# One run of filling products across both projections, with the split output weights in the places of x and h

## The chip, the cores and the metric

The kernel runs on one core of a Trainium2 chip. Its time is the device time of one execution, in microseconds (us). An execution under the profiler has a span, from the first instruction to the last, and a time of its own, somewhat longer.

The engines are named as the profile names them: PE (TensorE) for matrix products, with a granted clock that the profile shows; DVE (VectorE), ACT (ScalarE) and POOL (GpSimd) for the elementwise work; SP (SyncE), whose queue (SPq) issues nearly all DMAs here. Each engine works through its instructions in order.

## The reference

One layer of an encoder on 2048 tokens of width 1024: windowed attention with 16 query heads in 4 groups, then a SwiGLU part with 2816 hidden columns, each between two RMS norms and modulated by a vector c.

```python
mod = (c_act @ ada_w[i] + ada_b[i])[:, None, :]
sh1, sc1, g1, sh2, sc2, g2 = jnp.split(mod, 6, axis=-1)
h = rmsnorm(x, mix_norm_pre[i]) * (1.0 + sc1) + sh1
y = windowed_gqa_sink(h, att_w_qkv[j], att_w_o[j], att_sink[j], rel_bias)
x = x + g1 * rmsnorm(y, mix_norm_post[i])
h = rmsnorm(x, ffn_norm_pre[i]) * (1.0 + sc2) + sh2
y = swiglu(h, ffn_w_in[i], ffn_w_out[i])
x = x + g2 * rmsnorm(y, ffn_norm_post[i])
```

In windowed_gqa_sink, a block of 128 queries sees its own and the two neighbouring blocks of keys within 128 tokens; a learned sink logit per head joins the softmax; its output goes through w_o. All is computed to float32 accuracy: each operand is split into a high and a low part (hi, lo), and each product of two operands is three matmuls (hi by hi, hi by lo, lo by hi).

## The kernel before

Tokens come in four chunks of 512 (c = 0 to 3), each of four blocks of 128. The work has these stages.

**Front.** `Chunk` (L159) loads x of a chunk in eight tiles of 128 x 512, `squares` and `norm` make the reciprocal norm, and `h(k)` scales tile k by it (L196, DVE) and splits the result (hi L200 on ACT, lo L201 on DVE). Chunks 0 and 1 are projected to q, k and v (products psq and psv, L144 to L146) ahead of attention. `evac` (L205) takes a finished accumulator away (eq, on ACT and DVE) and SP writes it to DRAM (q_d, k_d, v_d). Between these, the modulation vector is made: `ada_load` brings a row of ada_w (tile ada, L271), `ada_reduce` (L275, DVE) multiplies it with c and sums.

**Attention.** 64 units (chunk, group, block), in the order of chunks, then groups. `Unit.scores` makes four score tiles s (L465, PE); DVE adds the bias and takes the negative row maximum nm (L468), ACT the exponential pr (L470), DVE the reciprocal rs (L472), POOL scales pr (L474). `Unit.values`, two units later (LAG), transposes pr (t, L487), splits it (phi on ACT, plo on DVE, L149 and L150) and multiplies by v (o, L492 and L493); ACT copies half of the result (low, L496), DVE adds (of, L497), SP writes it (o_d, L500). While a unit waits, PE has *filling*: products from a generator, of which `Budget.pull` (L733) draws so many per unit, FILL = 18 in units 0 to 31 and 17 in 32 to 63. `issue_after` lets them follow an instruction, here the first score of the unit before. In the first half `fill_qkv` (L503) projects chunks 2 and 3 (576 products; its weights wsr, L508, are split on ACT and POOL), and makes chunk 3's x, squares, norm and h on the way. In the second half `fillers_o` (L657) multiplies the finished attention outputs of chunks 0 to 2 by w_o: `TokenBlock` (L552) loads a block of o_d (tile ol, L558) and of x (xr, L563), splits ol, makes products py (L570 to L572), and then norms, residual and second norm (ysq, z, L576 to L584).

At unit 32 (L701 to L718) the first half's filling is drained, its pools are closed, pools for the second half are opened, and w_o is loaded in eight rows (wor, L714) and split (wo: hi on ACT, lo on DVE or POOL).

In units 8 to 31, two units of three load a row of ada_w (16 loads in all, L727), and the next unit reduces it.

**The last chunk.** `last_blocks` (L758) makes the four blocks of chunk 3's output projection, two at a time, in accumulators of the pool psC, which takes the place of attention's accumulators.

**Feed-forward.** 22 hidden tiles of 128 columns for two halves of the tokens, in seven products in place of eight for each 2 x 2 block (operands hb, ht, weights wa, ws, products pc_i, copies p_i L872), then the output products po (L1118 to L1120). It takes the rest of the time from about 790 us on.

A scheduler places the instructions: each engine's order follows a simulated timeline, in which an instruction may move ahead of where the code puts it, unless `issue_after` holds it. SP's queue keeps its order too.

Of the kernel before, what the change touches and what calls it, by code (L numbers as in the profile page):

```python
# [10 lines left out]
F32 = mybir.dt.float32  # L11
# [38 lines left out]
FILL = (18, 17)  # L50
LAG = 2

HOLD = 2
# [14 lines left out]
def encoder_layer(ctx, tc, a):  # L68
# [44 lines left out]
    def rstd_of(alloc, psp, ptag, acc, tag, r=None, direct=False):  # L113
# [8 lines left out]
        else:  # L122
            hi, lo = alloc(f"nhi{tag}")[:, :n].bitcast(F32R), alloc(f"nlo{tag}")[:, :n].bitcast(F32R)
# [28 lines left out]

    com = ExitStack()
    hs = open_pool(com, "hs", 12)
    ev = open_pool(com, "ev", 2)
    nrm = open_pool(com, "nrm")
    xs = open_pool(com, "xs", 8)

    class Chunk:  # L159


        def __init__(self, c):
            self.c, self.hh = c, [None] * KT
# [26 lines left out]
        def norm(self, psp, ptag):  # L190
            r = nrm.tile([P, CH], F32, tag="nr", name=f"nr{self.c}")
            self.r = rstd_of(rot(nrm, "nsq", 4), psp, ptag, self.acc, f"a{self.c}", r)

        def h(self, k):
            xt, c = self.xt[k], self.c
            scaled = dve.scalar_tensor_tensor(xt, xt, coef[:, 0, k:k + 1], self.r, ALU.mult, ALU.mult).ins  # L196
            hi = hs.tile([P, CH], F32R, tag="hi", name=f"hi{c}_{k}")
            lo = hs.tile([P, CH], F32R, tag="lo", name=f"lo{c}_{k}")
# [6 lines left out]
    def evac(c, n, ps, psp, ptag):  # L205

        if n < KT:
# [8 lines left out]
            dve.scalar_tensor_tensor(lo, src, DH ** -0.5, f(hi), ALU.mult, ALU.subtract)  # L216
# [27 lines left out]
    with ExitStack() as pa:  # L244
# [13 lines left out]
        cs = nrm.tile([KT, P], F32, name="cs")  # L258
# [5 lines left out]
        cb = nrm.tile([P, D], F32, name="cb")  # L264
# [91 lines left out]
        for i, n in enumerate(NORD):  # L356
# [13 lines left out]
            if i == 0:  # L370
# [7 lines left out]
                tb = nrm.tile([HEADS, CH], F32, tag="nacc", name="tb")[:, :RLEN]  # L378
# [124 lines left out]
    def fill_qkv(ch, nxt):  # L503

        for i, n in enumerate([8, 9, 10, 11] + list(range(8))):
# [12 lines left out]
            if nxt is not None:  # L518
# [33 lines left out]
    class TokenBlock:  # L552


        def __init__(self, c, b, pl=None, lo=pool):
            self.c, self.b, self.u = c, b, f"{c}_{b}"
            t = (pl or op).tile([P, 2, KT, P], F32R, tag="o", name=f"ol{self.u}", bufs=2)
            sp.dma_start(f(t[:, 1]), o_d[c][b])  # L558
            flat = t.rearrange("p s k t -> p s (k t)")
            split(flat[:, 0], flat[:, 1], f(flat[:, 1]), lo)  # L560
            self.o = t
            self.x = yq.tile([P, D], F32, tag="x", name=f"xr{self.u}", bufs=2)
            sp.dma_start(self.x, a["x"][c, b])  # L563
# [3 lines left out]
        def product(self, ps, i, k):  # L567
            w = wo_s[k][:, :, i * CH:(i + 1) * CH]
            o = self.o[:, :, k]
            pe.matmul(ps, o[:, 0], w[:, 0], start=k == 0, stop=False)  # L570
            pe.matmul(ps, o[:, 0], w[:, 1], start=False, stop=False)  # L571
            pe.matmul(ps, o[:, 1], w[:, 0], start=False, stop=k == KT - 1)  # L572
# [84 lines left out]
    def fillers_o():  # L657
        before = None
        for c in range(NCH - 1):
# [6 lines left out]
            before = turns(c, blocks) if c < CPH else None  # L666

# [26 lines left out]
    fill = Budget(fillers_qkv())  # L694
    load_qkv(0, 0)
    load_bias(0)
    oend = ExitStack()
    attn = ExitStack()
    wo_s = []
    for i, un in enumerate(units):  # L700
        if i == half:  # L701
            fill.drain()
            dve.tensor_tensor(coef[:, 1, :], mod[:, 16:24], gains[:, 1, :], ALU.mult)
            dve.scalar_tensor_tensor(coef[:, 2, :], mod[:, 32:40], 1.0, gains[:, 2, :], ALU.add, ALU.mult)
            com.close()
            wop = open_pool(oend, "wop")
            op = open_pool(oend, "op")
            yq = open_pool(oend, "yq")
            nq = open_pool(attn, "nq")
# [556 lines left out]
```

## Time and profile before

| | |
|---|---|
| times of three runs | 2108.52, 2105.21, 2102.14 us |
| median | 2105.21 us |
| the profiled execution: its time, its span | 2105.69, 2103.9 us |
| its granted PE clock, mean | 0.982 |
| stages of the span: front, attention, last chunk, feed-forward | to 173, to about 744, to 790, to 2104 us |

In the rows of a timeline stand the start, the duration, the engine, the line, the operation, the tiles (out<-in), the count, and in brackets how long the engine stood idle before and what it then waited for. A matmul's duration is longer than the distance of two matmuls, since they overlap. Rows of equal kind that follow each other are put together (x8).

### The profile page before, as it was taken

To read this page: it belongs to the slowest core of one execution; us is meant where nothing else is said; L and a number is where in the kernel's file an instruction comes from. 1 tells how busy PE (TensorE), PEld (TensorE's weight loads), DVE (VectorE), ACT (ScalarE), POOL (GpSimd) and SP (SyncE) were. 2 spreads that over 40 slices of the span, in tenths; PEclk is the share of its full clock that TensorE was granted. 3 is DMA by queue.
4 is the path that set the end of the run, shared out by engine and by line. 5 is a ranking of instruction groups with operands and counts; after the bars stand their busy time and mean duration, and the time that the engine had idled before them with its cause. 6 is when DMAs were issued, how large, how long until landed. Compare 5 with 4: busy or idle time off the path is not lost.

```text
span 2103.9 us, 28722 instructions
## 1 busy us (share of the span) xinstructions
PE 2025.3 (96%) x9400; PEld 1668.0 (79%) x9400; DVE 1504.8 (72%) x2616; ACT 1012.0 (48%) x2121; POOL 967.2 (46%) x930
## 2 busy tenths in 40 slices
PE   8999989989999999999999999999999999999998
PEld 5787777878878777888788887888888778877886
DVE  7755686677677668555575698777875689987677
ACT  4425666676777656333333344434333654435222
POOL 0305544555446543555555456555453242395340
PEclk9999999999999999999999999999999999999999
DMA  8788767764546575444642454544434454469763
GB/s 304 218 255 254 219 190 235 225 196 155 191 150 220 184 250 201 141 136 145 221 140 97 158 179 149 194 145 181 159 146 160 166 183 139 129 249 364 265 247 123
DMA packets 256405, 403.21 MB, mean 192 GB/s; under 512 B 84677, under 2 KB 135413, under 8 KB 254208
## 3 DMA queue, kind: packets, MB, share of 16 engines
q1 hardware_dynamic: 248992, 380.33, 54.2%
q10 hardware_dynamic: 5792, 16.79, 2.0%
q0 software_dynamic: 1472, 4.27, 0.5%
q8 instruction: 74, 1.21, 0.2%
q14 instruction: 75, 0.61, 0.1%
HBM read 268.36 MB, written 132.95 MB: 191 GB/s over the span
## 4 chain that ended last, share of the span: by engine, by line
PE 74%; DVE 9%; DMA 6%; POOL 4%; issue 3%; ACT 3%; SPq 1%; ACTq 0%; DVEq 0%; POOLq 0%
PE pc_i L145 12%; PE pc_i L146 12%; PE pc_i L144 12%; PE po L1119 5%; PE po L1120 5%; PE po L1118 5%; PE psq L144 3%; PE psq L146 3%; PE psq L145 3%; PE py L570 2%; PE py L571 2%; PE py L572 2%; PE t L487 2%; PE s L465 2%; DMA ada<-ada_w 1%
## 5 line engine op out<-in xcount | busy, mean ns | idle before, releaser
L146 PE MATMUL pc_i<-ht,ws_i 128*128 128x512 f32 x528 | 206.5, 391 | 0.0
L145 PE MATMUL pc_i<-ht,ws_i 128*128 128x512 f32 x528 | 206.4, 391 | 0.0
L144 PE MATMUL pc_i<-ht,ws_i 128*128 128x512 f32 x528 | 205.6, 390 | 0.0
L474 POOL TENSOR_SCALAR pr<-pr,rs 128x288 f32<-128x288 f32 (+3 forms) x256 | 131.8, 534 | 138.8 <-DVE rs L472 134.7
L470 ACT ACTIVATE pr<-pr,nm 128x289 f32<-128x289 f32 (+3 forms) x256 | 135.0, 529 | 76.7 <-DVE nm L468 66.2
L149 ACT CAST wa_i<-wiri 128x512 fp32r<-128x512 f32 x132 | 81.8, 621 | 182.0 <-PE pc_i L146 150.4
L468 DVE CUSTOM_DVE_ANT_0 pr<-s,bias,nsink 128x288 f32<-128x288 f32 (+3 forms) x256 | 124.4, 499 | 60.5 <-PE s L465 47.8
L808 POOL TENSOR_TENSOR s_i<-wiri 128x512 f32<-128x512 f32 x44 | 61.3, 1392 | 202.4 <-DMA wiri<-w_in 183.7
L150 DVE TENSOR_TENSOR ws_i<-s_i,ws_i 128x512 fp32r<-128x512 f32 x132 | 114.1, 864 | 40.9 <-ACT ws_i L149 40.6
L145 PE MATMUL pc_i<-hb,wa_i 128*128 128x512 f32 x352 | 138.5, 394 | 0.0
L150 DVE TENSOR_TENSOR plo<-t,phi 128x512 fp32r<-128x512 f32 x184 | 121.5, 681 | 23.3 <-ACT phi L149 23.0
L146 PE MATMUL pc_i<-hb,wa_i 128*128 128x512 f32 x352 | 138.1, 392 | 0.0
L144 PE MATMUL pc_i<-hb,wa_i 128*128 128x512 f32 x352 | 137.3, 390 | 0.0
L465 PE MATMUL s<-k,q 128*128 128x288 f32 (+4 forms) x512 | 112.1, 318 | 19.2 <-DVE nm L468 18.0
L150 DVE TENSOR_TENSOR wa_i<-wiri,wa_i 128x512 fp32r<-128x512 f32 x132 | 118.7, 900 | 15.3 <-ACT wa_i L149 14.8
L1118 PE MATMUL po<-wo_s,g 128*128 128x512 f32 x320 | 124.8, 394 | 4.8 <-ACT wo_s L149 4.0
L1119 PE MATMUL po<-wo_s,g 128*128 128x512 f32 x320 | 126.3, 395 | 3.1 <-DVE wo_s L150 3.1
L149 ACT CAST ws_i<-s_i 128x512 fp32r<-128x512 f32 x132 | 81.8, 620 | 98.3 <-PE pc_i L146 91.7
L1120 PE MATMUL po<-wo_s,g 128*128 128x512 f32 x320 | 125.9, 394 | 0.0
L487 PE MATMUL t<-ident,pr 128*128 128x128 f32 x736 | 112.6, 277 | 9.9 <-POOL pr L474 4.1
L1126 DVE TENSOR_TENSOR z<-po,z 128x512 f32<-128x512 f32 x140 | 94.4, 684 | 30.5 <-PE po L1120 29.0
L145 PEld LDWEIGHTS pc_i<-ht,ws_i 128*128 128x128 f32 x528 | 99.1, 188 | 21.6
(249 smaller groups left out, 6026.5 us busy)
## 6 DMA issues: line engine op xcount, KB each, us to landing
wiri<-w_in SPq DMA_DIRECT2D x88, 512.0 KB, 4.6
ada<-ada_w SPq DMA_DIRECT2D x40, 512.0 KB, 6.8
wr<-w_out SPq DMA_DIRECT2D x20, 1024.0 KB, 7.2
g<-g_d_t SPq DMA_DIRECT2D x36, 512.0 KB, 5.7
g<-g_d_b SPq DMA_DIRECT2D x35, 512.0 KB, 5.5
q_d<-eq SPq DMA_DIRECT2D x64, 256.0 KB, 4.8
q<-q_d SPq DMA_DIRECT2D x16, 1024.0 KB, 5.7
wsr<-w_qkv SPq DMA_DIRECT2D x24, 512.0 KB, 5.4
```

The costliest lines, as they stand in the source:

```text
L144: pe.matmul(ps, w[0], h[0], start=first, stop=False)
L145: pe.matmul(ps, w[0], h[1], start=False, stop=False)
L146: pe.matmul(ps, w[1], h[0], start=False, stop=last)
L149: act.copy(hi, src)
L150: return eng.tensor_tensor(lo, src, f(hi), ALU.subtract).ins
L465: m = pe.matmul(ps[:, :n], qs, kk[:, e, jb * P + lo:jb * P + hi], start=e == 0, stop=e == 1)
L470: act.activation(pr[:, i, lo:hi + 1], pr[:, i, lo:hi + 1], AF.Exp, bias=nm[:, i:i + 1], scale=-1.0, accum_out=rs[:, i:i + 1])
L474: pool.tensor_scalar(pr[:, i, lo:hi], pr[:, i, lo:hi], rs[:, i:i + 1], 1.0, ALU.mult, ALU.mult)
L487: pe.transpose(pt[:, i * P:(i + 1) * P], pr[:, i, jj * P:(jj + 1) * P], ident)
L1118: pe.matmul(ps, g[:, 0], w[:, 0], start=k == 0, stop=False)
L1119: pe.matmul(ps, g[:, 0], w[:, 1], start=False, stop=False)
L1120: pe.matmul(ps, g[:, 1], w[:, 0], start=False, stop=k == m - 1)
```

## The change

- **Places.** The pools xs (x) and hs (h) stay open after the first half. x of a chunk lies in two tiles of four, h in pairs (12 of them). The split output weights take these places: of w_o's columns 0 to 511 (half 0) four rows of tiles go where x was and four into h's pairs; of columns 512 to 1023 (half 1) all go into h's pairs. The pool op, opened at the start, first holds the squares, the norm and c's row.
- **When.** `output_weights` loads and splits half 0, a step per unit from unit 24 on. `filling` is one generator for both halves: the projection of chunks 2 and 3, then half 1's weights, then `fillers_o`. So there is no drain at unit 32. FILL is 17.9 everywhere; products follow the first score of two units before (SLACK = 2).
- **ada.** The 16 loads go out in units 8 to 23, one each; a row is reduced when two are outstanding, the older first.
- **Scalings.** Those of chunk 3 are held behind the evacuation just made (newest["evac"]).
- **Last chunk.** Its blocks 0 and 1 are loaded into tiles of their own (apart) behind units 62 and 63, and become filling; `last_blocks` makes blocks 2 and 3 only. `TokenBlock` loads x when the block's first product is evacuated (`begin`).

The core of the diff:

```diff
-FILL = (18, 17)
+FILL = 17.9
 LAG = 2
-
-HOLD = 2
+SLACK = 2
+HOLD = 1
...
-            self.xt = [xs.tile([P, CH], F32, tag="x", name=f"x{c}_{k}") for k in range(KT)]
+            groups = [xs.tile([P, 4, CH], F32, tag="x", name=f"x{c}_{i}") for i in range(2)]
+            self.xt = [groups[k // 4][:, k % 4] for k in range(KT)]
...
-                    nxt.h(2 * i - 16)
-                    nxt.h(2 * i - 15)
+                    with tc.issue_after(newest["evac"]):
+                        nxt.h(2 * i - 16)
+                        nxt.h(2 * i - 15)
...
+            if apart:
+                t = [nq.tile([P, D], F32, tag="n", name=f"ol{self.u}_{i}", bufs=5).bitcast(F32R) for i in range(2)]
+            else:
+                t = op.tile([P, 2, D], F32R, tag="o", name=f"ol{self.u}")
+                t = [t[:, 0], t[:, 1]]
+            sp.dma_start(f(t[1]), o_d[c][b].rearrange("p k t -> p (k t)"))
+            split(t[0], t[1], f(t[1]), lo)
+            self.o = [i.rearrange("p (k t) -> p k t", k=KT) for i in t]
...
+        for x in final:
+            yield from x.fill()
+
+    def proj_raw(i, m):
+        raw = ada_late.tile([P, D], F32, tag="raw", name=f"wor{i}_{m}").rearrange("p (e c) -> p e c", e=2)
+        sp.dma_start(raw, a["w_o"][2 * m:2 * m + 2, :, i * CH:(i + 1) * CH].rearrange("e p c -> p e c"))
+        return i, m, raw
+
+    def proj_split(i, m, raw):
+        if i == 0 and m < 2:
+            w = xs.tile([P, 4, CH], F32, tag="x", name=f"wo{i}_{m}").bitcast(F32R)
+            split(w[:, :2].rearrange("p e c -> p (e c)"), w[:, 2:].rearrange("p e c -> p (e c)"),
+                  raw.rearrange("p e c -> p (e c)"), dve)
+            for e in range(2):
+                wo_s[i, 2 * m + e] = (w[:, e], w[:, 2 + e])
+            return
+        for e in range(2):
+            w = hs.tile([P, 2, CH], F32R, tag="h", name=f"wo{i}_{m}_{e}")
+            split(w[:, 0], w[:, 1], raw[:, e], (dve, pool)[e])
+            wo_s[i, 2 * m + e] = (w[:, 0], w[:, 1])
+
+    def output_weights():
+        raws_ = [proj_raw(0, 0), proj_raw(0, 1)]
+        yield
+        for i in range(4):
+            proj_split(*raws_.pop(0))
+            if i < 2:
+                raws_.append(proj_raw(0, 2 + i))
+            yield
 
...
+    def filling():
+        nonlocal yq, nq, g1row
+        yield from fillers_qkv()
+        dve.tensor_tensor(coef[:, 1, :], mod[:, 16:24], gains[:, 1, :], ALU.mult)
+        dve.scalar_tensor_tensor(coef[:, 2, :], mod[:, 32:40], 1.0, gains[:, 2, :], ALU.add, ALU.mult)
+        raws_ = [proj_raw(1, m) for m in range(2)]
+        for m in range(2, 4):
+            proj_split(*raws_.pop(0))
+            raws_.append(proj_raw(1, m))
+        for x in raws_:
+            proj_split(*x)
+        com.close()
+        yq = open_pool(oend, "yq")
+        nq = open_pool(attn, "nq")
+        g1row = yq.tile([P, D], F32, name="g1row")
+        make_row(coef[:, 1, :], g1row, yq.tile([P, CH], F32, tag="sq", name="growt0", bufs=1), 0)
+        yield from fillers_o()
...
-        if waiting:
-            ada_reduce(*waiting.pop())
-        if KT <= i < half and i % 3 != 1:
+        if len(waiting) > 1:
+            ada_reduce(*waiting.pop(0))
+        if KT <= i < 3 * KT:
             with tc.issue_after(newest["wsr"]):
                 waiting.append(ada_load(next(late_ada), ada_late))
+        elif waiting:
+            ada_reduce(*waiting.pop(0))
+        elif 3 * KT <= i < half:
+            next(weights, None)
...
-        fill.pull(FILL[i >= half], units[max(i - 1, 0)].first)
+        if i >= len(units) - LAG:
+            final.append(TokenBlock(NCH - 1, len(final), True))
+        fill.pull(FILL, units[max(i - SLACK, 0)].first)
...
-    last_blocks(range(2), op)
...
-    last_blocks(range(2, JB), op2)
+    last_blocks(range(LAG, JB))
```

What this does to the engines' orders at three places. The first is DVE where chunk 3's norm ends (nr before, normed after), in the middle of attention; x_0 to x_7 are that chunk's x, nm and pr belong to scores, plo and of to values. Before:

```order
L136 TENSOR_TENSOR nr_2819<-nr_2819,nta_2827 128x512
L150 TENSOR_TENSOR plo_2_2_2791<-t_2_2_2785,phi_2_2_2790 128x512
L196 SCALAR_TENSOR_TENSOR x_0_2310<-x_0_2310,coef,nr_2819 128x512
L196 SCALAR_TENSOR_TENSOR x_1_2311<-x_1_2311,coef,nr_2819 128x512
L196 SCALAR_TENSOR_TENSOR x_2_2312<-x_2_2312,coef,nr_2819 128x512
L196 SCALAR_TENSOR_TENSOR x_3_2313<-x_3_2313,coef,nr_2819 128x512
L196 SCALAR_TENSOR_TENSOR x_4_2314<-x_4_2314,coef,nr_2819 128x512
L196 SCALAR_TENSOR_TENSOR x_5_2315<-x_5_2315,coef,nr_2819 128x512
L196 SCALAR_TENSOR_TENSOR x_6_2316<-x_6_2316,coef,nr_2819 128x512
L196 SCALAR_TENSOR_TENSOR x_7_2317<-x_7_2317,coef,nr_2819 128x512
L468 ISA pr_1780,nm_2_2743<-s_2_1_2751,bias_1893,nsink 128x288
L468 ISA nm_2_2743 128x1
```

After, where x_0 and x_1 are tiles of four:

```order
L283 ISA ada_3109,mod<-ada_3109,normed,adab 128x1024
L283 ISA mod 128x1
L135 SCALAR_TENSOR_TENSOR squared<-nsta_2741,squared 128x512
L136 TENSOR_SCALAR squared<-squared 128x512
L225 SCALAR_TENSOR_TENSOR eq_2_2935<-psq_4_2758,eq_2_2935 128x16x32
L137 TENSOR_TENSOR normed<-normed,squared 128x512
L476 ISA pr_1714,nm_2_2566<-s_2_1_2574,bias_1828,nsink 128x288
L476 ISA nm_2_2566 128x1
L476 ISA pr_1714,nm_2_2566<-s_2_2_2579,bias_1828,nsink 128x288
L476 ISA nm_2_2566 128x1
L205 SCALAR_TENSOR_TENSOR x_0_2245<-x_0_2245,coef,normed 128x512 x2
L505 TENSOR_TENSOR of_1_2532<-o_1_2497,low_1_2531 64x4x128
```

Eight scalings in one run have become pairs, with scores' and values' rows between them; a reduction of ada (L283) stands among them.

The second is PE at units 31 to 33, where the filling passes from one projection to the other (t, s and o are attention's, py_0_0 is the first block of the output projection). Before, in units 32 and 33:

```order
L487 MATMUL t_3_2_5089<-ident,pr_1779 128x128 x4
L465 MATMUL s_0_2_5040<-k_0_4593,q_0_4591 128x288 x2
L465 MATMUL s_0_3_5045<-k_0_4593,q_0_4591 128x288 x2
L465 MATMUL s_0_0_5135<-k_0_4593,q_0_4591 128x288 x2
L465 MATMUL s_0_1_5140<-k_0_4593,q_0_4591 128x288 x2
L465 MATMUL s_0_2_5145<-k_0_4593,q_0_4591 128x288 x2
L487 MATMUL t_3_0_5162<-ident,pr_1780 128x128 x4
L465 MATMUL s_0_3_5150<-k_0_4593,q_0_4591 128x288 x2
L487 MATMUL t_3_1_5173<-ident,pr_1780 128x128 x4
L465 MATMUL s_0_0_5225<-k_0_4593,q_0_4591 128x288 x2
L492 MATMUL o_3_5066<-phi_3_0_5072,v_3_4198 128x512
```

After, in unit 31:

```order
L584 MATMUL py_0_0_5028<-wo_2_1_4535,ol_0_5024 128x512
L495 MATMUL t_3_0_4830<-ident,pr_1716 128x128
L585 MATMUL py_0_0_5028<-wo_2_1_4535,ol_0_5024 128x512
L586 MATMUL py_0_0_5028<-wo_2_1_4535,ol_0_5024 128x512
L584 MATMUL py_0_0_5028<-wo_3_0_4633,ol_0_5024 128x512
L473 MATMUL s_3_2_4813<-k_3_4121,q_3_4119 128x288 x2
L585 MATMUL py_0_0_5028<-wo_3_0_4633,ol_0_5024 128x512
L586 MATMUL py_0_0_5028<-wo_3_0_4633,ol_0_5024 128x512
L584 MATMUL py_0_0_5028<-wo_3_1_4636,ol_0_5024 128x512
L473 MATMUL s_3_3_4818<-k_3_4121,q_3_4119 128x288 x2
L585 MATMUL py_0_0_5028<-wo_3_1_4636,ol_0_5024 128x512
L495 MATMUL t_3_1_4841<-ident,pr_1716 128x128
```

Before, attention's own rows follow each other without a product; after, products stand between them.

The third is PE at the end of attention: the last values (o_3), and the last chunk's blocks (py_0_0 and py_0_1 of block 0, py_1_0 of block 1). Before:

```order
L570 MATMUL py_3_1_8464<-wo_5024,ol_3_8428 128x512
L571 MATMUL py_3_1_8464<-wo_5024,ol_3_8428 128x512
L493 MATMUL o_3_8340<-plo_3_0_8347,v_3_7510 128x512
L572 MATMUL py_3_1_8464<-wo_5024,ol_3_8428 128x512
L492 MATMUL o_3_8340<-phi_3_1_8357,v_3_7510 128x512
L493 MATMUL o_3_8340<-plo_3_1_8358,v_3_7510 128x512
L570 MATMUL py_0_0_8559<-wo_4989,ol_0_8543 128x512
L571 MATMUL py_0_0_8559<-wo_4989,ol_0_8543 128x512
L572 MATMUL py_0_0_8559<-wo_4989,ol_0_8543 128x512
L570 MATMUL py_0_1_8560<-wo_4989,ol_0_8543 128x512
```

After:

```order
L584 MATMUL py_0_1_8476<-wo_3_0_5001,ol_0_0_8155 128x512
L500 MATMUL o_3_8346<-phi_3_0_8352,v_3_7475 128x512
L501 MATMUL o_3_8346<-plo_3_0_8353,v_3_7475 128x512
L500 MATMUL o_3_8346<-phi_3_1_8363,v_3_7475 128x512
L501 MATMUL o_3_8346<-plo_3_1_8364,v_3_7475 128x512
L585 MATMUL py_0_1_8476<-wo_3_0_5001,ol_0_0_8155 128x512
L586 MATMUL py_0_1_8476<-wo_3_0_5001,ol_0_1_8156 128x512
L584 MATMUL py_0_1_8476<-wo_3_1_5004,ol_0_0_8155 128x512
L585 MATMUL py_0_1_8476<-wo_3_1_5004,ol_0_0_8155 128x512
L586 MATMUL py_0_1_8476<-wo_3_1_5004,ol_0_1_8156 128x512
L584 MATMUL py_1_0_8527<-wo_0_4328,ol_1_0_8253 128x512
L585 MATMUL py_1_0_8527<-wo_0_4328,ol_1_0_8253 128x512
```

Block 0 stood behind the last values before; now it stands ahead of them, and 29 products, the rest of block 0 and all of block 1's first accumulator, stand between them and block 2.

More of the change, by code (lines that the diff above doesn't have):

```diff
@@ L150, in split, with square_at @@
         return eng.tensor_tensor(lo, src, f(hi), ALU.subtract).ins
+    oend = ExitStack()
     com = ExitStack()
-    hs = open_pool(com, "hs", 12)
+    xs = open_pool(oend, "xs", 2)
+    hs = open_pool(oend, "hs", 12)
+    op = open_pool(oend, "op", 2)
     ev = open_pool(com, "ev", 2)
-    nrm = open_pool(com, "nrm")
-    xs = open_pool(com, "xs", 8)
+    squared = op.tile([P, 4, CH], F32, tag="o", name="squared")
+    normed = op.tile([P, 4, CH], F32, tag="o", name="normed")
+    cb = normed.rearrange("p a b -> p (a b)")[:, :D]
+    turn_of_square = iter(range(10 ** 6))
+    def square_at():
+        return squared[:, next(turn_of_square) % 4]
     class Chunk:
@@ L567, in product @@
         def product(self, ps, i, k):
[L568 to L572, printed above, removed]
+            w = wo_s[i, k]
+            hi, lo = (t[:, k] for t in self.o)
+            pe.matmul(ps, hi, w[0], start=k == 0, stop=False)
+            pe.matmul(ps, hi, w[1], start=False, stop=False)
+            pe.matmul(ps, lo, w[0], start=False, stop=k == KT - 1)
         def evac(self, ps, i):
+            if i == 0:
+                self.begin()
             sq = yq.tile([P, CH], F32, tag="sq", name=f"ysq{self.u}_{i}", bufs=1)
@@ L693, in encoder_layer @@
     half, done = len(units) // 2, 0
-    fill = Budget(fillers_qkv())
     load_qkv(0, 0)
     load_bias(0)
-    oend = ExitStack()
     attn = ExitStack()
-    wo_s = []
-    for i, un in enumerate(units):
[L701 to L709, printed above, removed]
-            g1row = yq.tile([P, D], F32, name="g1row")
-            make_row(coef[:, 1, :], g1row, yq.tile([P, CH], F32, tag="sq", name="growt0", bufs=1), 0)
-            for k in range(KT):
-                raw = yq.tile([P, D], F32, tag="z", name=f"wor{k}", bufs=3)
-                sp.dma_start(raw, a["w_o"][k])
-                w = wop.tile([P, 2, D], F32R, name=f"wo{k}")
-                split(w[:, 0], w[:, 1], raw, (dve, pool)[k % 2])
-                wo_s.append(w)
-            fill = Budget(fillers_o())
+    wo_s, final = {}, []
+    def filling():
[15 more added lines that the diff above has]
+        yield from fillers_o()
+    yq = nq = g1row = None
+    fill = Budget(filling())
+    weights = output_weights()
+    for i, un in enumerate(units):
         un.scores()
@@ L756, in temp, with last_blocks @@
         return tmp.tile([P, CH], F32, tag=tag, name=name, bufs=bufs)
-    def last_blocks(bs, pl):
-        blocks = [TokenBlock(NCH - 1, b, pl) for b in bs]
+    def last_blocks(bs):
+        blocks = [TokenBlock(NCH - 1, b) for b in bs]
         ps = {(x, i): psC.tile([P, CH], F32, tag="p", name=f"py{x.u}_{i}") for x in blocks for i in range(2)}
```

32 lines of the change are left out of this document (13 added, 19 removed).

## The prediction, made before the changed kernel had run

> **What bounds the kernel now.** I read the page's first part, then the list of waits of TensorE (PE), then PE's timeline at each of its longer pauses up to 820 us, and beside it the engine that ended the pause.
>
> ```profile
> span 2103.9 us, 28722 instructions
> ...
> PE 2025.3 (96%) x9400; PEld 1668.0 (79%) x9400; DVE 1504.8 (72%) x2616; ACT 1012.0 (48%) x2121; POOL 967.2 (46%) x930
> ```
>
> PE is the bound: the next engine, VectorE (DVE), is busy for 72%. The change leaves the number of products as it is, so it can only win or lose what PE spends beside them: 78.6 us of pauses (2103.9 less 2025.3), and what its clock loses. The first row of PE's waits (columns: us in total, times, longest) says that scores waiting for DVE's row maxima are the largest of these:
>
> ```profile
> PE s L465 <- DVE nm L468: 18.0, 13, 5.3
> ```
>
> A pause costs more than itself when the clock falls behind it. PE's timeline behind two pauses:
>
> ```profile
> 468.10 0.41 PE L487 MATMUL t<-ident,pr 128*128 128x128 f32 x2 [1.08 <-DVE rs L472]
> ...
> 469.28 0.40 PE L570 MATMUL py<-wo,ol 128*128 128x512 f32 x1
> 469.51 0.39 PE L571 MATMUL py<-wo,ol 128*128 128x512 f32 x1
> ...
> 744.07 0.80 PE L570 MATMUL py<-wo,ol 128*128 128x512 f32 x1 [4.62 <-DVE of L497]
> ...
> 745.09 0.63 PE L572 MATMUL py<-wo,ol 128*128 128x512 f32 x1
> 745.52 0.63 PE L570 MATMUL py<-wo,ol 128*128 128x512 f32 x1
> ...
> 749.79 0.56 PE L571 MATMUL py<-wo,ol 128*128 128x512 f32 x1
> ```
>
> At full clock products start 0.23 us apart (469.28, 469.51). Behind 744.07 they start 0.43 apart (745.09, 745.52) until 749.79: 5.7 us for work of 5.7 × 0.23 / 0.43 = 3.1. So this pause cost 4.6 + 2.6 = 7.2 us. Where slow products follow for a shorter stretch I charge half of that surcharge, 1.3, as an estimate.
>
> **The change part by part.** Chunk 3's scaling by its norm comes first. What DVE did, and PE's pause:
>
> ```profile
> 265.09 7.48 DVE L196 SCALAR_TENSOR_TENSOR x<-x,coef,nr 128x512 f32<-128x512 f32 x8
> ...
> 273.06 0.85 PE L465 MATMUL s<-k,q 128*128 128x288 f32 x2 [5.26 <-DVE nm L468]
> ...
> 276.44 0.63 PE L145 MATMUL psq<-lo,ws 128*128 128x512 f32 x1
> ```
>
> Eight scalings (7.48 us) stand ahead of one row maximum, PE waits 5.26 and is still slow (0.63 for a product) at 276.44: 5.3 + 2.6 = 7.9 us. The change holds each pair of scalings behind an evacuation, and DVE now has them two at a time, 2 × 0.94 = 1.9 us. Of the run of eight PE covered 7.48 − 5.26 = 2.2, more than a pair's 1.9. So I take all 7.9 as gain; if two of the four pairs still meet a maximum without that cover, for 1.9 each at most, it is 4.1.
>
> The late loads of modulation weights (tile ada) stop PE twice:
>
> ```profile
> 341.78 1.28 DVE L275 CUSTOM_DVE_ANT_0 ada<-ada,cb,adab 128x1024 f32<-128x1024 f32 x1 [2.87 <-DMA ada<-ada_w]
> ...
> 343.57 0.56 PE L465 MATMUL s<-k,q 128*128 128x288 f32 x2 [3.48 <-DVE nm L468]
> ...
> 401.43 2.44 DVE L275 CUSTOM_DVE_ANT_0 ada<-ada,cb,adab 128x1024 f32<-128x1024 f32 x1 [1.30 <-DMA ada<-ada_w]
> ...
> 404.37 0.53 PE L465 MATMUL s<-k,q 128*128 128x288 f32 x2 [2.36 <-DVE nm L468]
> ```
>
> DVE, which works in order, sits at a reduction whose load has not landed; behind it stand row maxima, and PE waits for these. Price: 3.5 + 1.3 = 4.8, and 2.4 + 1.3 = 3.6, together 8.4 us. Now the same 16 loads go out in 16 consecutive units, and two are outstanding before one is reduced, which helps. But in the new order the reductions still float ahead on DVE, and SyncE's queue gets more waits: ada loads that need a buffer which DVE must free stand ahead of chunk 3's key writes, of attention's outputs and of four output-weight loads in units 17 to 20. All that SyncE sends is behind such a load, the next group's q, k and v too, and DVE and PE wait for that. Bounds: no stop (a gain of 8.4), or five at 4.8 (a loss of 15.6). I take one stop, 4.8, the nearest row: gain 3.6.
>
> The hand-over between the projections: before, no product is drawn in units 31 to 33, while the output weights are split and PE has only attention's work. PE there, beside the 1.08 at 468.10 above:
>
> ```profile
> 460.49 1.09 PE L487 MATMUL t<-ident,pr 128*128 128x128 f32 x4 [2.60 <-DVE plo L150]
> ```
>
> With one slow stretch that is 2.6 + 1.1 + 1.3 = 5.0 us. In the new order 23 products stand in each of units 31 to 33, and three in unit 30. The splits, on ACT, DVE and POOL, go from the hole to units 18 to 31, under full filling. I leave 1.5 for the short unit 30: gain 3.5 (bounds 5.0, and 0 if the splits there delay a maximum as much as here).
>
> The end of attention stays thin: before, units 61 and 62 draw no product; after, 61 draws six and 62 none.
>
> ```profile
> 698.55 0.44 PE L487 MATMUL t<-ident,pr 128*128 128x128 f32 x2 [2.03 <-POOL pr L474]
> ...
> 705.38 0.45 PE L465 MATMUL s<-k,q 128*128 128x160 f32 x2 [1.68 <-DVE nm L468]
> 705.67 0.62 PE L570 MATMUL py<-wo,ol 128*128 128x512 f32 x1
> ```
>
> 2.0 + 1.7, with a surcharge at each, are 6.3 us. As 48 products more are drawn ahead of this stretch and the hole itself is only a little shorter, I take 2.0 as gain (0 to 6.3). The product at 705.67 is slow (0.62) behind a pause of 1.68. [...]
>
> The last chunk: before, its block 0 waits at 744.07 for an accumulator that DVE's last attention output frees; DVE waits for ACT, and ACT, in order, for a block's load.
>
> ```profile
> 717.06 0.58 SPq L500 DMA_DIRECT2D o_d<-of  x1
> ...
> 725.75 1.07 ACT L149 CAST ol<-ol 128x1024 fp32r<-128x1024 f32 x1
> ...
> 739.95 1.04 ACT L149 CAST ol<-ol 128x1024 fp32r<-128x1024 f32 x1 [4.14 <-DMA ol<-o_d]
> ```
>
> As filling, blocks 0 and 1 use the filling's accumulators, and 29 products (29 × 0.235 = 6.8 us) lie between the last values and block 2's first product, more than the 4.62 it waited. Late next is block 0's own load: from the write at 717.06 to the end of the cast at 726.82 are 9.8 us, and the new order has some 45 products (10.5 us) between its unit's last values and its own first product, with the evacuation ahead of the write still to come off. I leave 1.5 (0 to 4.6): gain 7.2 − 1.5 = 5.7.
>
> The start of the feed-forward part, and chunk 1's norm at the front of the kernel:
>
> ```profile
> 77.42 0.59 PE L127 MATMUL nsta<-nloa,ones 128*128 128x512 f32 x1 [1.45 <-DVE nloa L125]
> ...
> 812.16 0.79 PE L144 MATMUL pc_i<-hb,ws_i 128*128 128x512 f32 x1 [4.99 <-ACT p_i L872]
> ```
>
> At 812.16 the order on PE is the old one, blocks 2 and 3 still end just before, and ACT's copy p_i stands behind the same work and six weight casts: I give 1.0 (bounds −2 and 5). At 77.42 the norm's product moves behind more products of the first wave, but x, now grouped in larger tiles, is loaded later: 2.0 of 1.45 + 1.3 (bounds −2 and 2.8).
>
> What no row shows: waits of ACT for output-weight loads in units 18 to 31, of PE for half 1's weights, of loads for buffers that hold x or h. They can't be below zero, since each is new; above, by the stop at 343.57, 4.8 in each of three places, 14.4. I take one, 4.8, since each has two units or more of work as cover.
>
> Sum: 7.9 + 3.6 + 3.5 + 2.0 + 5.7 + 1.0 + 2.0 − 4.8 = 20.9. The profiled execution took 2105.7 us, 1.8 around its span, and 0.5 above the median of the runs shown: 2105.7 − 20.9 = 2085.
>
> **The rivals.** A is the forecast, 2085.
>
> B: the hand-over and the end give nothing. For it: the pauses at 460.49, 468.10, 698.55 and 705.38 end with DVE and POOL, whose work per unit stays, and block 0's own load may be as late as the accumulator was. Against it: elsewhere, with 18 products in a unit, such pauses are short; of the 18.0 us in 13 waits for maxima the four quoted make 12.8, and the other nine 0.6 each. Then 3.5, 2.0 and 5.7 go: 2096.
>
> C, slower: SyncE's queue is held in units 8 to 31 by loads whose buffer is freed by a reduction or a split that is itself behind attention's work on DVE. The forecast counts two stops of 4.8. It is even at 20.9 / 4.8 = 4.4 stops more, slower by over 0.3% from six more; with ten in these 24 units it is 2085 + 8 × 4.8 = 2123. For it: one load in every unit where before two in three had one, and wo's loads behind them in the same queue. Against it: of 16 such loads two stopped PE before, and a second outstanding load gives each one unit more.
>
> D: the new waits don't come, and ada never stops PE: 20.9 + 4.8 + 4.8, and 3.0 of what is left in unit 30 and for block 0, is 33.5: 2072.
>
> That the change doesn't do what it says is excluded for filling and scalings by the order of instructions.
>
> **How the numbers follow.** A 0.64, B 0.17, C 0.07, D 0.12. The likeliest gives 2085. About 0.3%, 6.3 us, is what a measurement of this kernel can tell from no change; so 2099 is the line. A and D lie below it but for a little of A (its unknown costs at their upper end), and of B some two thirds: faster 0.84. Same is the rest of B, and some of A: 0.09. Slower is C: 0.07. The range reaches from D, with 2 more of the end's bound, to a little beyond B: 2070 to 2101.
>
> **What would show it.** Right: no run of eight scalings on DVE and no pause over 2 us near 273; no pause of PE over 1.5 us in units 31 to 33; block 2's first product without a wait for attention's accumulator; at most one stop over 3 us behind a reduction of ada. Wrong: scores waiting for row maxima still at 15 us or more in sum, with reductions or splits waiting for loads just ahead; a wait of over 4 us for block 0's load; a pause at the first products of half 1's weights; or a first wave that waits for x.

## The result, and the profile after the change

The change made the kernel slower, where the prediction had it faster. The changed kernel takes 2121.43 us, median of 5 runs (2114.2 to 2123.55); the kernel before takes 2105.21 (2102.14 to 2108.52). The ratio is 1.0067, 95% interval 1.0043 to 1.0091. The profiled execution took 2115.18 us, 1.9 of it around its span. Of all executions here, one of e3's twelve below stands apart at 6184.57 us, and its ratio is made without it. The page's first part:

```profile
span 2113.3 us, 28683 instructions
...
PE 2016.2 (95%) x9400; PEld 1661.8 (79%) x9400; DVE 1506.2 (71%) x2620; ACT 1009.4 (48%) x2127; POOL 969.9 (46%) x932
```

PE has the same 9400 products and is still the bound. What it spends beside them grew from 78.6 us to 97.1 (2113.3 − 2016.2).

Five of PE's waits in the changed kernel (us in total, times, longest):

```profile
PE nsta L127 <- DVE nhla L125: 15.0, 1, 15.0
PE pc_i L145 <- ACT p_i L925: 13.0, 2, 10.6
PE s L473 <- DVE nm L476: 9.5, 10, 2.9
PE t L495 <- DVE plo L151: 6.6, 2, 3.4
PE py L584 <- ACT ol L150: 3.1, 1, 3.1
```

Scores waiting for row maxima, the largest wait before, fell from 18.0 to 9.5. Two waits took their place that are not in attention at all: one of 15.0 at chunk 1's norm (1.45 before) and one of 10.6 at the start of the feed-forward part (4.99 before).

Where that leaves the time can be read from PE's first product of each stage, in us from the span's start:

| | before | after | stage longer or shorter |
|---|---|---|---|
| first score (front ends) | 171.9 | 190.7 | +18.8 |
| first feed-forward product (attention and last chunk end) | 790.4 | 795.7 | −13.5 |
| its 97th product | 820.6 | 830.9 | +5.0 |
| end of the span | 2103.9 | 2113.3 | −0.9 |

These rows add up to 9.4 us between the two profiled executions; the medians are 16.2 apart, since the changed kernel's profiled execution was the second fastest of five. Attention and the last chunk gave 13.5 of the 17.9 us that the prediction's terms for them make (7.9 + 3.6 + 3.5 + 2.0 + 5.7 − 4.8). The front took 18.8, and the start of the feed-forward part 5.0.

**The front.** PE and DVE in the changed kernel, where chunk 1's norm is made:

```profile
100.06 1.28 DVE L283 CUSTOM_DVE_ANT_0 ada<-ada,normed,adab 128x1024 f32<-128x1024 f32 x1 [5.97 <-DMA ada<-ada_w]
...
101.40 0.43 DVE L125 CAST nhla<-normed 128x512 fp32r<-128x512 f32 x1
...
101.88 0.79 PE L127 MATMUL nsta<-nhla,ones 128*128 128x512 f32 x1 [15.00 <-DVE nhla L125]
...
106.74 0.63 PE L146 MATMUL psq<-h,w 128*128 128x512 f32 x1
107.71 0.39 PE L146 MATMUL psq<-h,w 128*128 128x512 f32 x1
```

The sum of squares is cast into the tile nhla at 101.40; PE waits 15.0 us for that, and its products are slow (0.63 each, starting 0.43 us apart, at a granted clock of 0.50) until 107.4, 5.5 us; at the distance of 0.23 that they have from 107.48 on (clock 1.00), that is an estimated surcharge of 2.6. Together that is 17.6, where the kernel before waited 1.45: some 16 of the front's 18.8. SyncE's queue ahead of it:

```profile
74.71 7.46 SPq L238 DMA_DIRECT2D k_d<-e  x8
82.27 11.18 SPq L230 DMA_DIRECT2D q_d<-eq  x8
93.54 0.91 SPq L279 DMA_DIRECT2D ada<-ada_w  x1
94.55 3.22 SPq L346 DMA_DIRECT2D v_d<-e_v  x4
```

In the diff, `rstd_of` takes nhla (its two halves) as a tile of the tag "e" from the pool of evacuations. That tag has two buffers, which the keys and values of the first wave use in turn. The buffer that nhla gets is the one of the first values (e_v), and it is free when the first two of the writes v_d have read it; these are issued from 94.55 on, since eight key writes and eight query writes stand ahead of them, 18.6 us of issuing, and land 5.6 us after their issue (median of the four). A reduction of ada, whose load stands in the same place of the queue, ends on DVE just ahead of the cast, at 101.34; so in this run two late transfers end almost together.

**The start of the feed-forward part.** PE and ACT in the changed kernel, and then its SyncE queue:

```profile
815.74 0.62 ACT L150 CAST wa_i<-wiri 128x512 fp32r<-128x512 f32 x1 [2.20 <-DMA wiri<-w_in]
...
820.19 0.62 ACT L150 CAST ws_i<-s_i 128x512 fp32r<-128x512 f32 x1 [1.67 <-POOL s_i L862]
...
822.80 0.57 ACT L925 COPY p_i<-pc_i 128x512 f32<-128x512 f32 x1
823.42 0.80 PE L145 MATMUL pc_i<-hb,ws_i 128*128 128x512 f32 x1 [10.65 <-ACT p_i L925]
```

```profile
789.31 6.63 SPq L577 DMA_DIRECT2D xr<-x  x2
796.04 7.35 SPq L845 DMA_DIRECT2D ht<-hd_d_t  x12
803.90 5.02 SPq L845 DMA_DIRECT2D hb<-h_d  x4
809.02 0.38 SPq L856 DMA_DIRECT2D wiri<-w_in  x1
```

The same place in the queue of the kernel before:

```profile
766.93 0.33 SPq L803 DMA_DIRECT2D wiri<-w_in  x1
...
782.29 5.27 SPq L563 DMA_DIRECT2D xr<-x  x2
787.65 8.43 SPq L792 DMA_DIRECT2D ht<-hd_d_t  x12
```

Hidden tile 1's weights (wiri) were sent for at 766.93, 15 us ahead of x and the operands of the first level. In the changed kernel they stand behind all of these, at 809.02 (why was read from the code alone: the operands' loads have a raised priority, and the weights' memory seems to come free later). On ACT their casts are ahead of the copy p_i, and PE waits 10.65 for that copy.

**Attention.** The pairs of scalings, POOL and PE at two places of the changed kernel (of the other two pairs, the one at 299.61 reads the same, with 3.53; the one at 281.46 takes 2.68):

```profile
309.40 3.81 DVE L205 SCALAR_TENSOR_TENSOR x<-x,coef,normed 128x512 f32<-128x512 f32 x2
309.86 2.80 POOL L151 TENSOR_TENSOR ws<-wsr,ws 128x1024 fp32r<-128x1024 f32 x1
...
315.17 0.76 PE L495 MATMUL t<-ident,pr 128*128 128x128 f32 x4 [3.20 <-DVE plo L151]
...
323.62 3.51 DVE L205 SCALAR_TENSOR_TENSOR x<-x,coef,normed 128x512 f32<-128x512 f32 x2
324.00 2.58 POOL L151 TENSOR_TENSOR ws<-wsr,ws 128x1024 fp32r<-128x1024 f32 x1 [0.61 <-ACT ws L150]
```

Three of the four pairs take 3.5 to 3.8 us and not 1.9: POOL's split of a weight tile starts inside it. PE has no wait at 273 any more, but 3.20 and 3.40 us soon behind two of the pairs.

**The last chunk.** ACT and PE at its third block:

```profile
769.90 1.06 ACT L600 ACTIVATE xr<-z 128x1024 f32<-128x1024 f32 x1 [6.53 <-DVE z L599]
...
775.86 1.04 ACT L150 CAST ol<-ol 128x1024 fp32r<-128x1024 f32 x1
...
776.96 0.80 PE L584 MATMUL py<-wo,ol 128*128 128x512 f32 x1 [3.13 <-ACT ol L150]
```

The wait of 4.62 for an accumulator is gone. A wait of 3.13 for block 3's own operand has come: its cast stands on ACT behind an activation that waited 6.53 for DVE.

### The profile page after: what moved, and what is told of

It is laid out like the page before. It is cut to its first block, busy times and chain, and to the rows that moved or that the text cites. A ratio compares the mean times of both kernels' runs of the same rounds, so it can differ in the third digit from the quotient of the medians.

```text
span 2113.3 us, 28683 instructions
## 1 busy us (share of the span) xinstructions
PE 2016.2 (95%) x9400; PEld 1661.8 (79%) x9400; DVE 1506.2 (71%) x2620; ACT 1009.4 (48%) x2127; POOL 969.9 (46%) x932
## 4 chain that ended last, share of the span: by engine, by line
PE 66%; DMA 6%; DVE 5%; POOL 3%; issue 2%; ACT 2%; SPq 0%; DVEq 0%; POOLq 0%; ACTq 0%
PE pc_i L147 12%; PE pc_i L146 12%; PE pc_i L145 12%; PE po L1170 4%; PE po L1171 4%; PE po L1169 4%; PE t L495 3%; PE s L473 2%; PE py L584 2%; PE py L586 2%; PE py L585 2%; PE o L500 1%; PE o L501 1%; DMA wr<-w_out 1%; PE psq L145 1%
## 5 line engine op out<-in xcount | busy, mean ns | idle before, releaser
L146 PEld LDWEIGHTS pc_i<-ht,ws_i 128*128 128x128 f32 x528 | 99.4, 188 | 21.6
L145 PEld LDWEIGHTS pc_i<-ht,ws_i 128*128 128x128 f32 x528 | 99.4, 188 | 21.5
```

Of the source, the lines that this page charges most:

```text
L145: pe.matmul(ps, w[0], h[0], start=first, stop=False)
L146: pe.matmul(ps, w[0], h[1], start=False, stop=False)
```

## Experiments

The letters stand for theories. H: the halves' place in the evacuations' buffers costs the front its 15 us and what follows. W: the weights of hidden tile 1, behind other loads, cost the feed-forward part's start. S: the scalings' pairs collide with POOL's splits, so that spreading them gains nothing. A: reductions of ada that wait on DVE for their loads cost more than the few long stops show. X: x loads of the last chunk, ahead in SyncE's queue, make block 3's operand late. The expectations set rivals against them. Each ratio is to runs of the kernel before on the same chip; e1 to e4, e5 to e8 and e9 to e12 ran on three chips, so runs of different groups are compared by their ratios.

**e1, the halves in buffers of their own** (the changed kernel, otherwise as it is):

```diff
-            halves = ev.tile([P, 2, CH], F32R, tag="e", name=f"nhl{tag}")
-            hi, lo = halves[:, 0], halves[:, 1]
+            hi = ev.tile([P, CH], F32R, tag="nhi", name=f"nhi{tag}", bufs=1)
+            lo = ev.tile([P, CH], F32R, tag="vt", name=f"nlo{tag}", bufs=1)
```

> The changed kernel, with the two halves of the chunk norm's sum of squares in tiles of their own in place of a pair that rotates with the key and value evacuations (tag e). Theory H (the halves wait for a place that the value writes of chunk 0 free, and these stand in SP's queue behind eight query writes): PE's pause of 15.0 us at chunk 1's norm falls under 2 us, the slow clock behind it goes, and the time falls by 14 to 18 us, to about 2105. Rival R (the pause comes from the grouped x tiles, or from the reduction of ada that DVE does just ahead): the pause stays above 8 us, and the time within 6 us of the changed kernel's 2121.

2103.39 us (2096.37 to 2107.3), ratio to the kernel before 0.9989 (0.9976 to 1.0001). PE has no wait for the norm's halves left; the first score comes at 174.4 instead of 190.7. One tile's place was worth 16 us at the first score, and without it the loss of time is gone. The front stays 2.5 us later than before the change.

**e4, the reverse: the kernel before, with only the halves' tile moved to "e"**:

```diff
-            hi, lo = alloc(f"nhi{tag}")[:, :n].bitcast(F32R), alloc(f"nlo{tag}")[:, :n].bitcast(F32R)
+            halves = ev.tile([P, 2, CH], F32R, tag="e", name=f"nhl{tag}")
+            hi, lo = halves[:, 0], halves[:, 1]
```

> The kernel before with one part of the change alone: the halves of the norm's sum rotate with the key and value evacuations. Theory H: chunk 1's norm stops PE for 10 us or more (1.45 in the kernel before), and the time rises by 10 to 18 us, to about 2119. Rival R (grouped x tiles or the reductions): no pause over 4 us there, and the time stays within 5 us of 2105.

2123.19 us (2118.63 to 2125.05), ratio 1.0075 (1.0046 to 1.0104). The first score comes at 189.9 (171.9 before), and PE's row:

```profile
101.58 0.80 PE L127 MATMUL nsta<-nhla,ones 128*128 128x512 f32 x1 [17.43 <-DVE nhla L125]
```

This edit alone, without the new ada loads or the tiles of four, makes 16 to 18 us (by the ratio and by the medians). That the tile's place costs this is shown from both sides. What holds the cast, once the place is taken, is two things at once: three reductions of ada, which stood behind the cast in the kernel before (it at 73.83, they from 96.25), stand ahead of it in e4 and end at 101.01, and the second write that frees the buffer lands at 101.0. In the changed kernel too both end together. The place brings both, and no run parts them.

**e2, hidden tile 1's weights sent for ahead of the operands** (the changed kernel):

```diff
+    with tc.high_priority(offset=100):
+        ahead["i0_1"] = raw_load(wi[1], K2, "i0_1", a["w_in"][1], a["w_in"][HT + 1])
     with tc.high_priority(offset=100):
         half.load("t3", "t1", "t4", "b22")
```

> The changed kernel, with the weight load of the second hidden tile issued ahead of the twelve ht and four hb loads at the start of the feed-forward part. Theory W (ACT's copy p_i stands behind casts of weights whose load SP issues only after these): PE's pause before the first product that waits for p_i falls from 10.65 to 5 us or less, as in the kernel before, and the time by 4 to 6 us, to about 2116. Rival: the weights' sums on POOL, or the copy's place on ACT, keep the pause above 8 us, and the time stays at 2121.

2112.42 us (2110.14 to 2118.52), ratio 1.0041 (1.0025 to 1.0057). PE at the feed-forward part's start:

```profile
805.43 0.49 PE L145 MATMUL pc_i<-ht,ws_i 128*128 128x512 f32 x1 [2.12 <-ACT ht L150]
...
807.70 0.73 PE L146 MATMUL pc_i<-ht,ws_i 128*128 128x512 f32 x1 [1.77 <-DVE ht L151]
...
822.54 0.80 PE L145 MATMUL pc_i<-hb,ws_i 128*128 128x512 f32 x1 [3.02 <-ACT p_i L933]
```

The wait for p_i fell from 10.65 to 3.02, as W says, but the operands (ht), now behind the weights, are waited for instead: the first 96 products take 36.6 us, 35.2 in the changed kernel and 30.2 before. So the place of the weights made that one wait, but the stage is no shorter without it (35.2 to 37.6 us in the changed kernel, e1 and e12, which lack this edit): what lengthens it by 5.0 stays open. The interval overlaps the changed kernel's (1.0043 to 1.0091); that e2 is faster is likely, not shown.

**e3, e1's and e2's edits together** (the repaired kernel from here on):

> Both edits in the changed kernel: halves of their own, and the second hidden tile's weights ahead. If both theories hold, the two costs add: 2121 less 16 less 5 is 2100, some 5 us below the kernel before. By the rival of the first the time stays above 2112.

2100.53 us median (eleven of its twelve executions from 2096.38 to 2110.36), ratio 0.9978 (0.9963 to 0.9993): faster than the kernel before by 0.2%. By its stages attention and the last chunk take 602.1 us (780.4 − 178.3), 16.4 less than before: nearly the 17.9 forecast. The front is 6.4 later, the first 96 feed-forward products 5.5 longer. Two stops behind reductions of ada that the changed kernel didn't have are here (in e1 too, 4.51 and 3.93). DVE's and PE's rows:

```profile
293.99 2.38 DVE L283 CUSTOM_DVE_ANT_0 ada<-ada,normed,adab 128x1024 f32<-128x1024 f32 x1 [4.06 <-DMA ada<-ada_w]
...
298.72 0.72 PE L473 MATMUL s<-k,q 128*128 128x160 f32 x2 [4.51 <-DVE nm L476]
...
345.87 3.37 DVE L283 CUSTOM_DVE_ANT_0 ada<-ada,normed,adab 128x1024 f32<-128x1024 f32 x1 [4.99 <-DMA ada<-ada_w]
...
349.73 1.09 PE L473 MATMUL s<-k,q 128*128 128x288 f32 x3 [4.04 <-DVE nm L476]
```

**e5, the kernel before, with only the scalings in pairs behind an evacuation**:

```diff
+                    with tc.issue_after(newest["evac"]):
+                        nxt.h(2 * i - 16)
+                        nxt.h(2 * i - 15)
```

> The kernel before with one part of the change alone: chunk 3's scalings held behind the evacuations, two at a time. The prediction's term: the pause of 5.26 us at 273 and its slow stretch go, the time falls by 7.9 us, to about 2097. Theory S (a scaling reads two tiles from memory and stands still while POOL splits a weight tile, which comes beside each evacuation: pairs took 3.8 and 3.5 us in the changed kernel, where two free ones take 1.4 to 1.5): two or more pairs take over 2.6 us, PE pauses of 2 to 3.5 us stand there in place of the one, and the time falls by no more than 4 us.

2105.45 us (2096.25 to 2113.51), ratio 1.0008 (0.9994 to 1.0022). The largest term of the sum, 7.9 us, is nothing when made alone. Three of its pairs take 3.5 us or more, the last 1.39. DVE and POOL at the first:

```profile
271.74 3.56 DVE L196 SCALAR_TENSOR_TENSOR x<-x,coef,nr 128x512 f32<-128x512 f32 x2
272.12 2.62 POOL L150 TENSOR_TENSOR ws<-wsr,ws 128x1024 fp32r<-128x1024 f32 x1 [0.33 <-ACT ws L149]
```

The pair is slow beside POOL here too. The wait of 5.26 at 273 goes; waits of 1.92 (280.48) and 1.89 (292.02) stand between the pairs, one of 3.20 (260.25) 11 us ahead of the first, and the waits at attention's end are longer (3.10 and 2.73, where 2.03 and 1.68 were). That the slow pairs alone eat up the gain is therefore not shown.

**e6, the repaired kernel, the low parts of these weight tiles on DVE instead of POOL**:

```diff
-            split(w[:, 0], w[:, 1], raw, pool)
+            split(w[:, 0], w[:, 1], raw, dve if nxt is not None and i >= 8 else pool)
```

> The repaired kernel of the run with both edits, with the low parts of the four weight tiles beside these scalings made by DVE in place of POOL. Theory S: no scaling of chunk 3 takes over 1.0 us any more (2.83 us for a pair before), though DVE has four splits of about 1.2 us more; the time falls by 1 to 4 us from 2100. Rival (the long pairs come from something else, such as the loads): pairs of over 2.6 us remain.

2094.17 us (2091.58 to 2098.46), ratio 0.9955 (0.9942 to 0.9968). The first, second and fourth of its pairs (the third takes 1.65), and the split that POOL still makes beside the fourth:

```profile
265.87 1.41 DVE L205 SCALAR_TENSOR_TENSOR x<-x,coef,normed 128x512 f32<-128x512 f32 x2
281.17 1.41 DVE L205 SCALAR_TENSOR_TENSOR x<-x,coef,normed 128x512 f32<-128x512 f32 x2
...
305.48 3.51 DVE L205 SCALAR_TENSOR_TENSOR x<-x,coef,normed 128x512 f32<-128x512 f32 x2
305.86 2.59 POOL L151 TENSOR_TENSOR ws<-wsr,ws 128x1024 fp32r<-128x1024 f32 x1 [1.65 <-ACT ws L150]
```

1.41 to 1.65 where no split of POOL's runs beside, 3.5 where one does, in the same run: the collision is shown, though the expectation that no scaling is slow any more was missed. e3's four pairs took 2.83, 1.40, 1.40 and 3.51; at its second it was POOL's split, begun after the pair, that took longer (3.48). So the edit shortened one pair, by 1.4 us, and the gain of some 5 us has another part that wasn't found: the stops of 4.51 and 4.04 behind reductions aren't in e6's profile either. The interval touches e3's (0.9963 to 0.9993), and e10 below gains nothing from the same edit.

**e7, the repaired kernel, each reduction of ada held on DVE behind the last row maximum of its unit**:

```diff
-            ada_reduce(*waiting.pop(0))
+            with tc.issue_after(un.last):
+                ada_reduce(*waiting.pop(0))
```

> The repaired kernel with each late reduction of ada held behind the last row maximum of its unit, so that it can't move ahead to units before. Theory A of the prediction (a reduction that stands ahead of row maxima and waits for its load stops PE): the pauses of 4.5 us at 299 and 4.0 us at 350 and their slow stretches go, and the time falls by 6 to 12 us, to 2088 to 2094. Rival: a reduction waits as long behind the last maximum and stops the next unit's, so that pauses of 3 us or more remain, and the time stays within 3 us of 2100.

2082.51 us (2081.49 to 2085.95), ratio 0.9898 (0.9886 to 0.9911): by the ratios some 17 us below e3, well over the 6 to 12 expected. DVE's wait for these loads (us in total, times, longest) in e3 and then in e7:

```profile
DVE ada L283 <- DMA ada<-ada_w: 23.6, 12, 5.0
```

```profile
DVE ada L283 <- DMA ada<-ada_w: 13.4, 5, 5.2
```

The stops of 4.51 and 4.04 are gone; one of 3.02 remains, at 301.81, for plo. The work of each engine in attention's first half (stretch, its length; busy us and instructions of PE, PEld, DVE, ACT, POOL; granted clock; DMA share; GB/s), in e3 and then in e7:

```profile
175.00:465.00 290.00, 269.28 (x1402) 224.09 (x1401) 207.36 (x499) 192.89 (x465) 165.10 (x231) 0.96 0.73 218
```

```profile
175.00:465.00 290.00, 279.38 (x1473) 231.99 (x1473) 211.85 (x522) 200.98 (x488) 156.19 (x237) 0.98 0.77 229
```

In the same 290 us e7 gets 71 matmuls more done, at a granted clock of 0.98 instead of 0.96. Part of that is a front that ends 4.4 us sooner (the first score at 173.9, 178.3 in e3). The stretch from 310 to 440 us shows the rest best: 706 matmuls for 658, PE idle for 1.6 us and not 6.7, at a clock of 1.00 for 0.96.

**e9, the kernel before, with reductions held in the same way**:

> The kernel before, with each late reduction of ada held behind the last row maximum of its unit, and nothing else. Theory A: the two pauses of 3.48 and 2.36 us (8.4 us with their slow stretches) go, and the time falls by 5 to 9 us, to about 2097; as the repaired kernel fell by 18 us with the same edit, this says how much of that belongs to the change's own denser loads. Rival: the reductions wait behind the maxima instead, and the time stays within 3 us of 2104.

2090.54 us (2087.68 to 2091.38), ratio 0.9926 (0.9909 to 0.9943): 14.8 us. The prediction priced everything that ada cost this kernel at 8.4, by its two long stops. That holding the reductions back is worth more is shown, in both kernels. DVE's wait for the loads in the kernel before, and then in e9:

```profile
DVE ada L275 <- DMA ada<-ada_w: 25.3, 11, 3.6
```

```profile
DVE ada L275 <- DMA ada<-ada_w: 14.4, 6, 4.2
```

The two long stops (343.57 and 404.37) are gone. From 310 to 440 us e9 does 718 matmuls for 669, with PE idle for 1.4 us and not 5.8, at a clock of 1.00 for 0.97; at that pace 49 matmuls are some 9 us, about what the two stops were priced at. The other 6 of the 14.8 couldn't be put down to a wait: PE's waits for maxima make 19.1 us in 13 times in e9, 18.0 in 13 before, with new ones of 2.92 and 2.90 (264.64, 268.39) in the place of 5.26, and of 5.52 (452.31) at the hand-over.

**e8, the repaired kernel, the last chunk's x loads on POOL's queue**:

```diff
-            sp.dma_start(self.x, a["x"][self.c, self.b])
+            (pool if self.c == NCH - 1 else sp).dma_start(self.x, a["x"][self.c, self.b])
```

> The repaired kernel with the last chunk's x loads issued by POOL's queue in place of SP's. Theory X (the load of x for the last chunk's block 1, which moved to the first evacuation, waits for a buffer at the head of SP's queue, and the last attention output's write and block 3's load stand behind it): the pause of 3.3 us at block 3's first product goes, and the time falls by 3 to 6 us, to 2095 to 2098. Rival: the load or its cast on ACT is late on its own, and the pause stays over 2 us.

2099.14 us (2097.06 to 2103.61), ratio 0.9978 (0.9967 to 0.9989), as e3. ACT and PE at block 3:

```profile
756.65 1.06 ACT L600 ACTIVATE xr<-z 128x1024 f32<-128x1024 f32 x1 [6.54 <-DVE z L599]
...
762.00 1.04 ACT L150 CAST ol<-ol 128x1024 fp32r<-128x1024 f32 x1
...
763.09 0.50 PE L584 MATMUL py<-wo,ol 128*128 128x512 f32 x1 [3.41 <-ACT ol L150]
```

X has fallen: the wait is as long (3.41) with the x loads out of the way. The cast's place behind the activation that waits 6.54 for DVE, and behind seven other casts, is what is left; it was only read from the rows, no run moved it.

**e10, e7 with e6's edit; e11, e10 with e8's; e12, the changed kernel once more**, on one chip with e9:

> The repaired kernel with both the reductions held behind the last maximum and the low parts of the four weight tiles on DVE. If the two costs are apart, 2100 less 18 less 6 is 2076; if the shorter pairs of scalings only helped because reductions stood beside them, it stays at 2082.

> As the run before, and the last chunk's x loads by POOL's queue, so that SP's queue reaches the twelve ht loads sooner: the pause of 3.0 us of the fourth product (waiting for ht) at the start of the feed-forward part falls under 1.5 us, and the time by 2 to 4 us against the run before. Rival: ACT's casts are late on their own, no difference.

> The changed kernel again, on the chip of these runs, as the measure for the runs that undo one part: 2115 to 2123 us, with a pause of 13 us or more at chunk 1's norm.

e10: 2082.08 us, ratio 0.9893 (0.9872 to 0.9914), no better than e7: what the edit gained in e6 isn't there once the reductions are out of the way. e11: 2087.51, 0.9913 (0.9891 to 0.9934); a wait of PE for the first operands ht goes from 2.90 to 1.33, and the time isn't lower; the intervals overlap, so nothing follows. e12: 2117.93 (2115.4 to 2121.86), 1.0061 (1.0045 to 1.0077): the loss is there again, with a wait of 12.41 at the norm (13 or more was expected) and 9.14 for p_i.

## Why the prediction was wrong

**The front** is the step that failed. "2.0 of 1.45 + 1.3 (bounds −2 and 2.8)" asked when x comes and where the product stands among the wave's products. It did not ask what the diff's new tile for the halves shares its buffers with. That was to be read in the diff and in SyncE's queue of the profile before: the tag "e" rotates through buffers whose readers are writes, and these stand in a queue where the keys' and queries' writes alone take 18 us to issue:

```profile
70.99 7.50 SPq L229 DMA_DIRECT2D k_d<-e  x8
78.58 10.91 SPq L221 DMA_DIRECT2D q_d<-eq  x8
```

It measured −18.8, of which 16.3 go with e1's edit. Of what is left, the loss of 2.5 us in e1 and 6.4 in e3, no cause was shown; e6, e7 and e8, with the same edit, lose 2.0 to 3.1, so 3 to 4 us of e3's come from something else than the change. x in larger tiles is a candidate for the rest, and wasn't tried. The signs that the prediction named for being right all came (no run of eight scalings and no pause over 2 us near 273, 1.25 at most in units 31 to 33, no wait for attention's accumulator, no stop over 3 us behind a reduction): the loss lay where none of them looked.

**The feed-forward part's start** was given 1.0, with −2 as its lower bound, on the ground that PE's order is the old one. It is, but SyncE's isn't: weights that had gone out early stood behind 18 loads. It measured −5.0 in the changed kernel, and −5.5 in e3 with that wait cut to 3.02, so the weights' place isn't the whole of it; what else lengthens the stage, beside the waits for the operands ht, stays open.

**The scalings**, 7.9: wrong. The pair was sized 2 × 0.94 = 1.9 from a run of eight, a mean that hides one slow scaling among fast ones: among the 32 of the kernel before, the shortest took 0.740 us, the median 0.748 and the longest 2.844. Behind an evacuation POOL's split ran beside three pairs of four for most of their time, in the changed kernel and in e5, and these took 3.5 to 3.8. The bound of 4.1 assumed 1.9 as well. e5 measured no gain; how much of the 7.9 the slow pairs took away wasn't measured.

**ada**, 3.6 of 8.4: the mechanism was right, its size wrong. The changed kernel has no stop over 3 us behind a reduction; the repaired one has two, 4.5 and 4.0, since its front no longer delays attention while the loads arrive (argued from the two traces, not tried). And the sum counted only PE's stops of over 2 us. Holding the reductions back is worth 14.8 us in the kernel before and some 17 in the repaired one. The two long stops, with their slow stretches, account for some 9 of the 14.8; that shorter waits of DVE make the rest is a guess. Rival C forecast a slower kernel, by more long stops behind these loads; the kernel is slower, but the changed kernel has no such stop.

**The hand-over**, 3.5: as forecast on its pauses. The longest one in units 31 to 33 is now 1.25 us (at 489.88), under the 1.5 that was allowed, where 2.60 and 1.08 were. **The end of attention**, 2.0: pauses of 2.46 and 1.17 us remain, of 2.03 and 1.68 before, but the slow stretch behind them is gone (products take 0.39 to 0.40 there, where 0.63 stood behind 705.38), so a gain of about the surcharge that had been charged (2 × 1.3). **The last chunk**, 5.7: the accumulator's wait went; what is late next is not block 0's load but block 3's, 3.13 and slow products (0.43 apart, at a granted clock of 0.50) for 6.2 us behind it, an estimated surcharge of 2.9, against the 1.5 that was left. That makes 7.2 − 3.1 − 2.9 = 1.2. **The new costs**, 4.8: neither ACT nor PE has a long wait for output weights in units 18 to 31; they did not come where they were looked for.

The forecast for attention and the last chunk as a whole, 17.9, was close (13.5, and 16.4 in e3), but with terms that were each off; that is no proof of them. Between the profiled executions the whole sum missed by 30.3 (by the median, 2121 for 2085, it is 36): 20.8 at the front, 6.0 at the feed-forward part's start, 4.4 in between, less 0.9 behind.

The fastest kernels, e7 and e10, take about 2082 us, 1.0% below the kernel before; of that, late reductions alone give the old kernel 0.7% (e9).

## What to carry to other kernels

When a diff gives a small tile a new tag, list what else rotates through that tag and what must read it before the buffer is free: here a 4 KB-per-partition scratch tile waited for stores behind 16 other stores. Where PE's order is unchanged, still compare the order of the DMA queues: here a load that slipped behind 18 others was issued at 809.02 instead of 766.93, and PE waited 10.65 where it had waited 4.99. What a waiting instruction costs is priced more surely by holding it back in a run (14.8 us here) than by adding the two longest pauses it leaves on the bottleneck (8.4), and the duration of an operation that is moved is read beside its new neighbours (3.5 to 3.8 us for a pair here), not as a mean (1.9).

## What the runs showed of the hardware

A scaling of 128x512 on DVE, which reads two such tiles (x and nr), took 0.748 us by the median of the 32 in the kernel before. The one that began there at 269.1, with POOL's 128x1024 subtraction beside it (268.50, for 2.85), took 2.84. In e5 a pair at 271.74 took 3.56, with POOL's subtraction from 272.12 for 2.62; in e6, with that subtraction on DVE itself (1.22 us), the first two pairs took 1.41 each. The subtraction can be the longer one too: in e3 it took 3.48 from 281.93, beside a pair of 1.40 that had begun at 281.76, where the median of the 24 in the kernel before is 2.40. That the two get in each other's way is what these rows show; by what means, they don't.

What a pause costs through the clock varies. Behind 3.13 us at 776.96 in the changed kernel the products were slow for 6.2 us, and behind 3.20 and 3.40 at 315.17 and 329.00 for 3.8 and 3.4, at a granted clock of 0.50; behind 2.46 at 685.73 they weren't slow at all (clock 1.00). In the kernel before, 1.68 at 705.38 had 3.7 us of slow products behind it (0.52). The length of the pause alone doesn't order these cases.
